# A two-block fp32 model on one core: the cross-attention memory loaded features-first, its 1/rms moved to keys and values, and the second attention's values projected at the start

## The chip, the cores and the metric

The kernel runs on one core of a Trainium2 chip. The metric is the device time of one launch, in microseconds (us), the median of several executions. Lower is better.

## What is computed

A batch of one sequence of 256 tokens with 1024 features goes through two models in a row. The first is one block: adaptive modulation of a hybrid mixer (a state-space scan beside causal attention) and a feed-forward. The second has two layers, each with a SwiGLU feed-forward, a mixer (layer 0: trailing means, layer 1: native sparse attention, NSA), a cross-attention to a memory of 256 tokens, and another feed-forward. The change is about that memory, the input `mem_2` of 256 x 1024:

```python
def rms_norm_2(x, g):
    xf = x.astype(F32)
    y = xf * lax.rsqrt(jnp.mean(xf * xf, axis=-1, keepdims=True) + EPS)
    return (y * g.astype(F32)).astype(x.dtype)

def memory_cross_attention(h, mem_n, w_q, w_kv, w_o):
    q = (h @ w_q).astype(F32).reshape(B, S, Hx, dh) * dh ** -0.5
    k, v = jnp.split((mem_n @ w_kv).astype(F32), 2, axis=-1)
    p = jax.nn.softmax(jnp.einsum('bqhd,bkhd->bhqk', q, k), axis=-1)
    o = jnp.einsum('bhqk,bkhd->bqhd', p, v).reshape(B, S, D)
    return o.astype(h.dtype) @ w_o

for i in range(2):
    ...
    x = x + memory_cross_attention(rms_norm_2(x, xattn_norm[i]), rms_norm_2(mem, mem_norm[i]),
                                   xattn_w_q[i], xattn_w_kv[i], xattn_w_o[i])
```

The memory does not depend on `x`, so its keys K and values V of either layer (called K0, V0, K1, V1 here) can be computed at any time before they are used. The 1/rms of a memory token is one number per token; the gain `mem_norm` is one number per feature and layer. A factor per token passes through the projection `mem_n @ w_kv` unchanged.

## The kernel before

**fp32 as three products.** Every fp32 operand of a large matmul is split in two parts, hi (ACT, a cast, L183 for weights and L393 for activations) and lo (DVE or POOL, the difference, L184 and L394). A product is then three matmuls (hi by hi, lo by hi, hi by lo), all issued in `mm`, L232.

**Weights.** The class `Weights` (object `W`) holds the list of all weight tiles in the order of use. Each is 1 MB (128 x 2048), loaded by SP at L166 into one of four raw tiles `w`, and then split in four pieces of 128 x 512 into `hi` and `lo`. `W.get` hands out a tile and emits the loads and splits of the next two. The modulation's weights, `ada`, are not split: DVE multiplies them with a row of the conditioning (`crow`, in tile `xn`) and sums, two instructions of 128 x 1024 for each (L581).

**A granule** is here one weight tile of the memory's projection, 256 output columns over all 1024 features and 256 tokens: 48 matmuls of 128 x 256 into one PSUM bank of the pair `wk`. K of a layer is granules 0 to 3 of `xkv`, V is granules 4 to 7. `kv_proj` runs them and hands each result to a function `put`.

**The start.** SP loads the two halves of the memory tokens-first into `x0` and `x1` (L319), and then weight tiles in the order "KAKAKAKAAKAKAKAK" (K a granule of xkv, A one of ada). DVE sums squares by token (L539), POOL takes the power -1/2 (L542), DVE scales (L543), PE transposes 16 blocks (L401), and `gained` multiplies with layer 0's gain (L408) and splits into `memT[0]`. Then come K0's four granules; layer 1's gain is put on the same transposed blocks (`memT[1]`); then K1's four granules. `put` copies a granule out of PSUM on ACT (L569). The input `xT` is loaded behind the first granule of K1. Then the first block's input is modulated (L599, tile `A`) and its projections begin (tiles `hTh`, `hTl`, first matmul `ck<-hTh,m`).

**Spills.** K0, K1 and both `memT` pairs (four MB for these) go to DRAM in the first block, by DMAs on ACT's queue (`spill_mem`, `spill_more`, `spill_rest`), since their SBUF tiles are needed. In the first block stands also the matmul pair `ck<-aa,gt`, which takes the decays that DVE computes up to L727.

**Later uses.** POOL loads `memT[0]` back before the first mixer of the second model, where V0's four granules run (`v_keep`, ACT copies at L1324) beside the trailing means (L1302 to L1320). POOL loads `memT[1]` back (`mem_load(1)`) in NSA, and V1's four granules run there as a filler of the attention (`wk<-hi,s` and `wk<-lo,s`, ACT copies at L1572), with their four weight tiles.

**NSA.** For each of two groups `o_` run `nq_proj`, `compressed` and `branches`. `branches` has 8 heads; each has `scores` (12 matmuls with `acc` as output, row maxima on DVE at L1518 and L1519, exponentials on ACT) and, one head later, `values`: three transposes of the probabilities for each token half (L1537 to L1539, the first of the pairs is called T here), copies on ACT (L1540), 12 instructions `ck<-A,m` of 65 columns, and on DVE the scaling by the gates (L1548 to L1551). POOL adds the result to `on` (tile `A`, L1554 and L1555). `turned` transposes `on` (L1581) and splits it for the output projection `nwo`, whose first half has the two `nwo` tiles (outputs `wk`, added to `x` at L1594) and whose second half is `out_tail` (outputs `acc`).

**What sets the order.** The order of the instructions on each engine is fixed when the program is built. A scheduler in the build takes the instructions, their dependences and estimated costs, and puts matmuls that need nothing of the attention between its steps. PE cannot choose at run time: if the next matmul in its list waits, all behind it wait.

Of the kernel before, what the change touches and what calls it, by code (L numbers as in the profile page):

```python
# [9 lines left out]
F32 = mybir.dt.float32  # L10
# [3 lines left out]
OP = mybir.AluOpType  # L14
# [50 lines left out]
def lay_out(i):  # L65
# [4 lines left out]
    o["mem"] = np.ascontiguousarray(a["mem_2"][0])  # L70
# [128 lines left out]
def tile_model(ctx: ExitStack, tc: tile.TileContext, I, out):  # L199
# [80 lines left out]
    j = i = 0  # L280
    for ch in "KAKAKAKAAKAKAKAK":
        if ch == "K":
            add(f"xkv{j // 4}", j % 4, j % 4 + 1, I["xkv"][j // 4])
            j += 1
        else:
            add_ada(i)
            i += 1
# [23 lines left out]
    add("xkv1", 4, 8, I["xkv"][1])  # L311
# [207 lines left out]
    memd = [[dp.tile([P, 2048], F32, name=f"memd{l}{i}") for i in range(2)] for l in range(2)]  # L519
    memps = []  # L520
    memT = [pair_tile(("s8_0", "s8_1")), pair_tile(("s8_2", "s8_4"))]
    jk = sb("s8_4", [P, D], BF16)
# [25 lines left out]
    with tc.issue_after(last["hi"].ins), tc.issue_after(last["lo"].ins):  # L548
        W.emit(1)
# [14 lines left out]
    def k_hold(l):  # L564
        k_held.append([sb(f"x{h}", [P, 4, S]) for h in range(2)] if l == 0 else [sb("s8_3", [P, 8, S])])

        def put(j, ps):
# [76 lines left out]
    def spill(dst, src):  # L644
# [1016 lines left out]
```

## Time and profile before

| | us |
|---|---|
| median of 3 runs (lowest, highest) | 1628.38 (1624.29, 1629.59) |
| the profiled execution, as timed | 1626.63 |
| its span, first to last instruction | 1624.9 |
| PE busy | 1582.5 (97%) |
| DVE busy | 1063.9 (65%) |
| ACT busy | 836.6 (51%) |
| POOL busy | 261.5 (16%) |
| DMA traffic | 304.21 MB, mean 187 GB/s |
| mean granted TensorE clock | 0.993 of full |

The profiled execution lies 1.75 us under the median of the three. Times of instructions count from the start of the span. PE's busy time covers matmuls that overlap in the pipeline, so a matmul of 0.28 us may start every 0.12 us, and a short wait can hide in it; what counts on PE is the distance between starts. In a timeline the bracket at a row's end holds the idle time before it and what released it.

### The profile page before, as it was taken

The numbers are of one execution on the slowest core, as the hardware profiler recorded it, in microseconds if no ns is written. First come the engines' busy times: TensorE is split into PE (matmuls) and PEld (weight loads), VectorE is DVE, ScalarE is ACT, GpSimd is POOL, SyncE is SP. The second block draws the span as 40 slices with busy tenths as digits, with TensorE's granted clock in tenths as the row PEclk, the third lists the DMA queues.
The fourth block names the chain that finished last, engine by engine and source line by source line (L and its number), as shares of the span: only waits on it lengthen the run. The fifth ranks groups of instructions, "written<-read, shape, count | busy, mean of one in ns | idle before, by whom it ended". The sixth has DMA issues, their size and how long they took to land.

```text
span 1624.9 us, 29581 instructions
## 1 busy us (share of the span) xinstructions
PE 1582.5 (97%) x12110; PEld 1514.5 (93%) x12110; DVE 1063.9 (65%) x1938; ACT 836.6 (51%) x1720; POOL 261.5 (16%) x266
## 2 busy tenths in 40 slices
PE   7999999899999999999999999999999999999998
PEld 7999998798988999989999999999989999999897
DVE  8889977874548655586665457544678566575453
ACT  4565446364535544465554445443546675464442
POOL 2003002320301110130121012201200211022011
PEclk9999999999999999999999999999999999999999
DMA  8874766475545555524365545544445223365530
GB/s 321 335 290 154 295 249 221 151 278 203 182 156 208 208 182 208 182 104 182 130 227 188 183 156 208 182 182 156 178 171 207 79 104 131 130 222 185 197 136 27
DMA packets 43432, 304.21 MB, mean 187 GB/s; under 512 B 5008, under 2 KB 5264, under 8 KB 7328
## 3 DMA queue, kind: packets, MB, share of 16 engines
q1 hardware_dynamic: 39312, 283.66, 48.3%
q0 software_dynamic: 2112, 10.49, 1.8%
q10 hardware_dynamic: 1872, 8.17, 1.3%
q8 instruction: 95, 1.56, 0.4%
q14 instruction: 41, 0.34, 0.1%
HBM read 294.96 MB, written 7.34 MB: 186 GB/s over the span
## 4 chain that ended last, share of the span: by engine, by line
PE 62%; DVE 4%; ACT 2%; issue 1%; POOL 0%; POOLq 0%; DVEq 0%; ACTq 0%
PE wk L232 21%; PE ck L232 20%; PE acc L232 19%; DVE lo L184 1%; ACT hi L183 1%; DVE s L1411 0%; DVE m L1307 0%; PE ck L1537 0%; DVE hTl L1045 0%; PE ck L1538 0%; PE ck L1539 0%; ACT s L183 0%; DVE m L408 0%; PE ck L1265 0%; DVE hTl L394 0%
## 5 line engine op out<-in xcount | busy, mean ns | idle before, releaser
L183 ACT CAST hi<-w 128x512 fp32r<-128x512 f32 (+1 forms) x708 | 417.0, 644 | 406.5 <-issue 251.2
L184 DVE TENSOR_TENSOR lo<-w,hi 128x512 fp32r<-128x512 f32 (+1 forms) x708 | 496.8, 745 | 147.8 <-ACT hi L183 144.1
L232 PE MATMUL wk<-hTl,hi 128*128 128x256 f32 x992 | 281.3, 284 | 1.5 <-DVE hTl L1045 1.5
L232 PE MATMUL wk<-hTh,hi 128*128 128x256 f32 x992 | 282.5, 285 | 0.0
L232 PE MATMUL wk<-hTh,lo 128*128 128x256 f32 x992 | 281.1, 283 | 0.0
L394 POOL TENSOR_TENSOR A<-m,A 128x256 fp32r<-128x256 f32 x119 | 135.7, 1146 | 666.3 <-ACT A L393 653.2
L183 ACT CAST s<-w 128x512 fp32r<-128x512 f32 x224 | 126.1, 617 | 138.5 <-issue 85.3
L232 PEld LDWEIGHTS wk<-hTl,hi 128*128 128x128 f32 x992 | 187.5, 189 | 2.7 <-DVE hTl L1045 1.9
L232 PEld LDWEIGHTS wk<-hTh,hi 128*128 128x128 f32 x992 | 187.5, 189 | 0.9 <-issue 0.2
L232 PEld LDWEIGHTS wk<-hTh,lo 128*128 128x128 f32 x992 | 187.2, 189 | 0.1
L232 PE MATMUL acc<-A,hi 128*128 128x256 f32 x1024 | 185.2, 283 | 0.9 <-ACT A L393 0.9
L184 DVE TENSOR_TENSOR s<-w,s 128x512 fp32r<-128x512 f32 x224 | 146.3, 697 | 53.5 <-ACT s L183 51.6
L232 PEld LDWEIGHTS acc<-A,hi 128*128 128x128 f32 x1024 | 157.0, 189 | 1.4 <-ACT A L393 1.1
L232 PE MATMUL ck<-hTh,hi 128*128 128x256 f32 x528 | 149.1, 282 | 0.0
L232 PE MATMUL ck<-hTh,lo 128*128 128x256 f32 x528 | 148.7, 282 | 0.0
L232 PE MATMUL ck<-hTl,hi 128*128 128x256 f32 x528 | 148.7, 282 | 0.0
L232 PE MATMUL acc<-A,lo 128*128 128x256 f32 x512 | 143.3, 280 | 0.0
L232 PE MATMUL acc<-hi,A 128*128 128x512 f32 x432 | 139.9, 398 | 0.0
L232 PE MATMUL ck<-hTh,s 128*128 128x256 f32 x672 | 123.7, 282 | 0.0
L232 PEld LDWEIGHTS ck<-hTh,s 128*128 128x128 f32 x672 | 105.5, 190 | 0.0
L232 PEld LDWEIGHTS ck<-hTh,hi 128*128 128x128 f32 x528 | 99.5, 188 | 0.1
L232 PEld LDWEIGHTS ck<-hTl,hi 128*128 128x128 f32 x528 | 99.4, 188 | 0.1
(407 smaller groups left out, 3162.7 us busy)
## 6 DMA issues: line engine op xcount, KB each, us to landing
w<-in_ffn_i SPq DMA_DIRECT2D x88, 1024.0 KB, 4.8
w<-in_ffn_o SPq DMA_DIRECT2D x44, 1024.0 KB, 4.8
w<-in_ada SPq DMA_DIRECT2D x24, 1024.0 KB, 5.5
w<-in_win SPq DMA_DIRECT2D x22, 1024.0 KB, 7.1
w<-in_xkv SPq DMA_DIRECT2D x16, 1024.0 KB, 6.2
w<-in_ffi SPq DMA_DIRECT2D x16, 1024.0 KB, 4.8
w<-in_ffo SPq DMA_DIRECT2D x16, 1024.0 KB, 4.8
w<-in_nin SPq DMA_DIRECT2D x10, 1024.0 KB, 4.8
```

Source lines behind the costliest of these rows:

```text
L183: nc.scalar.copy(h[:, sl], t[:, sl])
L184: nc.vector.tensor_tensor(lo[:, sl], t[:, sl], h[:, sl].bitcast(F32), op=OP.subtract)
L232: T.matmul(o, lhsT=lhsT, rhs=rhs, start=start, stop=stop)
L394: i = (lo or V).tensor_tensor(dst[1], src, dst[0].bitcast(F32), op=OP.subtract)
```

## The change

`mem_2` is laid out features-first on the host and loaded as `mraw` (two DMAs of 512 KB into `hTh`). There are no transposes at the start. `mem_gain(l)` puts a layer's gain on it: for each of 8 feature blocks an ACT instruction of 128 x 256 (hi) and a DVE instruction (lo). `mem_sums` computes the 1/rms: two ACT squares of 128 x 1024, 16 one-column matmuls against ones, a DVE instruction, POOL's power into `mcol` (a column by token), two matmuls that turn it into a row in PSUM and an ACT copy into `mrow`. Keys are multiplied by the row when they leave PSUM (DVE, in place of the ACT copy), values by the column (two ACT instructions in place of one copy). The order at the start is K1, V1, K0, with 12 granules in place of 8 and the same 8 `ada` tiles. V1 is spilled to DRAM (`vd`) and loaded back by one POOL DMA where its projection stood in NSA. Of the memory only layer 0's pair is spilled.

```diff
@@ -67,7 +67,7 @@
-    o["mem"] = np.ascontiguousarray(a["mem_2"][0])
+    o["memT"] = np.ascontiguousarray(a["mem_2"][0].T.reshape(8, P, S).transpose(1, 0, 2)).reshape(P, 8 * S)
@@ -277,11 +277,12 @@
-    j = i = 0
-    for ch in "KAKAKAKAAKAKAKAK":
+    early = [("xkv1", j) for j in range(8)] + [("xkv0", j) for j in range(4)]
+    i = 0
+    for ch in "KKAKAKKAKAKAKAKKAKAK":
         if ch == "K":
-            add(f"xkv{j // 4}", j % 4, j % 4 + 1, I["xkv"][j // 4])
-            j += 1
+            name, j = early.pop(0)
+            add(name, j, j + 1, I["xkv"][int(name[-1])])
...
     add("nin", 6, 10)
-    add("xkv1", 4, 8, I["xkv"][1])
     add("nwo", 0, 4)
...
-    mt = [sb(f"x{t}", [P, D]) for t in range(2)]
-    for t in range(2):
-        nc.sync.dma_start(mt[t], I["mem"][TS[t]])
+    mraw = sb("hTh", [P, 8, S])
+    for h in range(2):
+        nc.sync.dma_start(mraw[:, 4 * h:4 * h + 4].rearrange("p k s -> p (k s)"), I["memT"][:, h * 1024:h * 1024 + 1024])
...
-    for t in range(2):
-        ss = stat(2)
-        V.scalar_tensor_tensor(jk, mt[t], 1.0, mt[t], op0=OP.mult, op1=OP.mult, accum_out=ss[:, 0:1])
-        ms, rs = stat(), stat()
-        V.tensor_scalar(ms, ss[:, 0:1], D * 1e-6, None, op0=OP.add)
-        G.tensor_tensor(rs, ms, mhalf, op=OP.pow)
-        V.tensor_scalar(mt[t], mt[t], rs, 32.0, op0=OP.mult, op1=OP.mult)
-    for t in range(2):
-        ps = transposes(mt[t], t)
-        gained(ps, t, memT[0], vec("mem_norm0"))
-        memps.append(ps)
...
+    def mem_gain(l):
+
+        for k in range(8):
+            g = vec(f"mem_norm{l}", k)
+            A.activation(memT[l][0][:, k], mraw[:, k], AF.Copy, scale=g)
+            V.scalar_tensor_tensor(memT[l][1][:, k], mraw[:, k], g, memT[l][0][:, k].bitcast(F32), op0=OP.mult, op1=OP.subtract)
+
+    mcol = cp.tile([P, 2], F32, name="mcol")
+    mrow = sb("rrow", [P, S], bufs=2)
+
+    def mem_sums():
+        sq = sb("hTl", [P, 8, S])
+        for h in range(2):
+            A.activation(sq[:, 4 * h:4 * h + 4], mraw[:, 4 * h:4 * h + 4], AF.Square)
+        ps = ck((P, 2))
+        for t in range(2):
+            for k in range(8):
+                mm(ps[:, t:t + 1], sq[:, k, TS[t]], ones[:, 0:1], start=k == 0, stop=k == 7)
+        ms = stat(2)
+        V.tensor_scalar(ms, ps, 1.0 / D, 1e-6, op0=OP.mult, op1=OP.add)
+        G.tensor_tensor(mcol, ms, mhalf.broadcast_to([P, 2]), op=OP.pow)
+        ps = ck((P, S))
+        for t in range(2):
+            mm(ps[:, TS[t]], mcol[:, t:t + 1].broadcast_to([P, P]), ident)
+        A.copy(mrow, ps)
+
+    mem_gain(1)
...
         def put(j, ps):
-            n = 4 // len(k_held[l])
-            A.copy(k_held[l][j // n if n < 4 else 0][:, 2 * (j % n):2 * (j % n) + 2], ps)
             if l == 1 and j == 0:
-                tc.keep_in_program_order(A.dma_start(xT, I["xT"].rearrange("p (k t) -> p k t", k=8)))
+                mem_sums()
+            n = 4 // len(tiles)
+            V.tensor_tensor(tiles[j // n if n < 4 else 0][:, 2 * (j % n):2 * (j % n) + 2], ps,
+                            mrow.unsqueeze(1).broadcast_to([P, 2, S]), op=OP.mult)
+        return put
+
+    def v_put(vt, after=None):
+        def put(j, ps):
+            for t in range(2):
+                A.activation(vt[:, t, (j - 4) * 256:(j - 4) * 256 + 256], ps[:, t], AF.Copy, scale=mcol[:, t:t + 1])
+            if after and j == 4:
+                after()
         return put
...
+    kv_proj(1, k_hold(1), 0, 4)
+    mem_gain(0)
+    v1 = A0([P, 2, D])
+    kv_proj(1, v_put(v1, lambda: tc.keep_in_program_order(A.dma_start(xT, I["xT"].rearrange("p (k t) -> p k t", k=8)))), 4, 8)
+    spill(kd[1], k_held[0][0])
+    spill(vd, v1)
     kv_proj(0, k_hold(0), 0, 4)
-    for t in range(2):
-        gained(memps[t], t, memT[1], vec("mem_norm1"))
-    kv_proj(1, k_hold(1), 0, 4)
...
-    spill_rest()
...
-    mem_load(1)
...
-    kv_proj(1, v1_keep, 4, 8)
+    G.dma_start(KV[1][1].rearrange("p t d -> p (t d)"), vd)
```

DVE at the start: L543 scales the memory, L408 and L394 make the gained pair, L581 (now L607) is the first `ada` step, `lo_199` (now `lo_150`) the first weight tile's lo parts. Before:

```order
L408 TENSOR_TENSOR m_30_192<-acc_171,vecs 128x256
L394 TENSOR_TENSOR s_1_6_111<-m_29_188,s_0_5_110 128x2x128
L581 SCALAR_TENSOR_TENSOR w_211,modc<-w_211,xn_117 128x1024
L184 TENSOR_TENSOR lo_199<-w_196,hi_198 128x512 x4
L184 TENSOR_TENSOR lo_216<-w_213,hi_215 128x512 x4
```

Now:

```order
L541 SCALAR_TENSOR_TENSOR s_4_7_111<-hTh_67,vecs,s_2_6_110 128x256 x8
L184 TENSOR_TENSOR lo_150<-w_147,hi_149 128x512 x4
L184 TENSOR_TENSOR lo_162<-w_159,hi_161 128x512 x4
L607 SCALAR_TENSOR_TENSOR w_171,modc<-w_171,xn_114 128x1024 x2
L555 TENSOR_SCALAR stat_242<-ck_225 128x2
L541 SCALAR_TENSOR_TENSOR s_1_5_109<-hTh_67,vecs,s_0_4_108 128x256 x3
```

The first `ada` step moved from ahead of the first granule's lo parts to behind the second's.

PE in NSA, in the attention heads of the first group, from a head's first T to the next head's values. L1537 to L1539 and their new numbers L1554 to L1556 are the transposes, `wk_14576` is V1's granule 4, `wk_14786` a part of the turned attention output. Before:

```order
L1537 MATMUL ck_13872<-ident,m_731_13824 128x128
L1538 MATMUL ck_13872<-ident,m_731_13824 128x128
L1539 MATMUL ck_13872<-ident,m_731_13824 128x128
L232 LDWEIGHTS identb
L232 MATMUL acc_13897<-negm,identb 128x2x128
L232 MATMUL wk_14576<-hi_14050,s_1_675_13392 128x256
L232 MATMUL wk_14576<-hi_14050,s_0_674_13391 128x256
L232 MATMUL wk_14576<-lo_14051,s_0_674_13391 128x256
```

Now:

```order
L1554 MATMUL ck_14168<-ident,m_731_14120 128x128
L1555 MATMUL ck_14168<-ident,m_731_14120 128x128
L1556 MATMUL ck_14168<-ident,m_731_14120 128x128
L232 LDWEIGHTS identb
L232 MATMUL acc_14193<-negm,identb 128x2x128
L1595 MATMUL wk_14786<-ident,A_624_13067 128x128 x2
L1554 MATMUL ck_14173<-ident,m_731_14120 128x128
```

Behind the last row of the piece before come 15 more matmuls of V1 and then the head's second T; now there are one or two transposes of the turned output, or nothing, between the two T. The next piece is DVE in attention heads without V1: L1519 (now L1536) is the row maximum of the wider scores of the next head, L1551 (now L1568) the scaling that frees the `ck` bank which the second T writes. Before, in a head of the second group:

```order
L1518 TENSOR_REDUCE stat_14376<-acc_14368 128x2
L1548 RECIPROCAL rv_14319<-ck_14312 128x4
L1549 TENSOR_TENSOR rv_14319<-rv_14319,gates_12866 128x4
L1551 TENSOR_TENSOR m_823_14322<-ck_14312,rv_14319 128x256
L1519 TENSOR_REDUCE stat_14376<-acc_14369 128x2
```

Now, in a head of the first group:

```order
L1535 TENSOR_REDUCE stat_14116<-acc_14108 128x2
L184 TENSOR_TENSOR lo_14796<-w_14793,hi_14795 128x512
L1565 RECIPROCAL rv_14059<-ck_14052 128x4
L1536 TENSOR_REDUCE stat_14116<-acc_14109 128x2
L1566 TENSOR_TENSOR rv_14059<-rv_14059,gates_13082 128x4
L184 TENSOR_TENSOR lo_14796<-w_14793,hi_14795 128x512
L1568 TENSOR_TENSOR m_717_14062<-ck_14052,rv_14059 128x256
```

The maximum has moved ahead of the scaling, as in four of the first group's heads.

## Rows read from the trace of the kernel before

**Rows 1.** The page of the profile: busy time by engine (us, share of the span, instructions), and the share of the span of each engine in the chain that ended last.

```profile
PE 1582.5 (97%) x12110; PEld 1514.5 (93%) x12110; DVE 1063.9 (65%) x1938; ACT 836.6 (51%) x1720; POOL 261.5 (16%) x266
...
PE 62%; DVE 4%; ACT 2%; issue 1%; POOL 0%; POOLq 0%; DVEq 0%; ACTq 0%
```

**Rows 2.** What PE waited for over the whole span: the waiting output and line, the releaser, us in total, times, longest.

```profile
PE wk L232 <- ACT hi L183: 3.7, 1, 3.7
PE wk L232 <- DVE lo L184: 3.3, 3, 1.7
PE acc L232 <- ACT hTh L1317: 2.6, 1, 2.6
...
PE ck L232 <- DVE x L727: 1.5, 1, 1.5
```

**Rows 3.** Stretches of the span: from:to, length, busy us of PE, PEld, DVE, ACT and POOL (instructions), granted clock, DMA share, GB/s.

```profile
10.00:20.00 10.00, 4.92 (x28) 4.24 (x28) 10.00 (x21) 7.10 (x16) 3.92 (x4) 0.85 0.81 339
...
20.00:68.00 48.00, 46.32 (x389) 45.96 (x389) 46.87 (x84) 25.89 (x49) 4.52 (x4) 1.00 0.97 373
```

**Rows 4.** PE's timeline from the first granule to the end of K1: start, us, line, operation, idle time before it.

```profile
15.61 0.51 PE L232 MATMUL wk<-s,hi 128*128 128x256 f32 x2 [3.71 <-ACT hi L183]
17.45 0.58 PE L232 MATMUL wk<-s,lo 128*128 128x256 f32 x1 [1.33 <-DVE lo L184]
...
20.39 0.40 PE L232 MATMUL wk<-s,hi 128*128 128x256 f32 x2
...
43.70 0.39 PE L232 MATMUL wk<-s,lo 128*128 128x256 f32 x1 [1.68 <-DVE lo L184]
...
66.08 0.28 PE L232 MATMUL ck<-hTh,m 128*32 128x256 f32 x1
```

**Rows 5.** The timelines of ACT and of DVE at the start.

```profile
14.95 4.25 ACT L183 CAST hi<-w 128x512 fp32r<-128x512 f32 x8
15.06 1.21 DVE L581 SCALAR_TENSOR_TENSOR w<-w,xn 128x1024 f32<-128x1024 f32 x1
16.20 3.00 DVE L184 TENSOR_TENSOR lo<-w,hi 128x512 fp32r<-128x512 f32 x4
```

**Rows 6.** ACT's copies of the first four granules, each started when its granule's last matmul had ended.

```profile
24.54 0.59 ACT L569 COPY x<-wk 128x512 f32<-128x512 f32 x1 [5.34 <-PE wk L232]
30.30 0.59 ACT L569 COPY x<-wk 128x512 f32<-128x512 f32 x1 [2.79 <-PE wk L232]
```

**Rows 7.** Groups of instructions in the first 75 us, shapes kept apart: count, busy us, mean ns of one, idle before.

```profile
L184 DVE TENSOR_TENSOR lo<-w,hi 128x512 fp32r<-128x512 f32 x32 | 20.9, 714 | 0.5 <-ACT hi L183 0.5
L581 DVE SCALAR_TENSOR_TENSOR w<-w,xn 128x1024 f32<-128x1024 f32 x16 | 19.9, 1281 | 0.0
...
L408 DVE TENSOR_TENSOR m<-acc,vecs 128x256 f32<-128x256 f32 x16 | 5.9, 411 | 0.0
...
L542 POOL TENSOR_TENSOR stat<-stat,mhalf 128x1 f32<-128x1 f32 x2 | 1.1, 566 | 4.3 <-DVE stat L541 4.3
```

**Rows 8.** The DMAs issued between 1.5 and 2.0 us on SP's queue: transfers, KB each, us from issue to landing.

```profile
w<-in_xkv SPq DMA_DIRECT2D x1, 1024.0 KB, 9.9
x<-in_mem SPq DMA_DIRECT2D x1, 512.0 KB, 6.1
```

**Rows 9.** PE's timeline around the decays of the scan.

```profile
114.56 0.40 PE L232 MATMUL ck<-aa,gt 128*128 128x16 f32 x2 [1.49 <-DVE x L727]
114.81 0.37 PE L232 MATMUL ck<-aa,le 128*128 128x16 f32 x2
...
116.15 0.42 PE L232 MATMUL wk<-lo,hTh 128*128 128x256 f32 x1
...
119.35 0.29 PE L232 MATMUL wk<-lo,hTh 128*128 128x256 f32 x1
```

**Rows 10.** ACT's timeline where V0 is projected: instructions of the trailing means, and one copy of V0.

```profile
704.20 0.51 ACT L1320 ACTIVATE x<-x,psb 128x256 f32<-128x256 f32 x1
...
706.40 0.57 ACT L1324 COPY s<-wk 128x512 f32<-128x512 f32 x1
```

**Rows 11.** PE's timeline in NSA: the first T of heads with V1 between (1262.31, 1293.36) and without (1319.08, 1322.80), a second T (1324.09), and the first matmul behind the last values of the first group (1296.47).

```profile
1262.31 0.28 PE L1537 MATMUL ck<-ident,m 128*128 128x128 f32 x1
...
1293.36 0.28 PE L1537 MATMUL ck<-ident,m 128*128 128x128 f32 x1
...
1296.47 1.03 PE L232 MATMUL ck<-kc,s 128*128 128x32 f32 x8
...
1319.08 0.28 PE L1537 MATMUL ck<-ident,m 128*128 128x128 f32 x1
...
1322.80 0.28 PE L1537 MATMUL ck<-ident,m 128*128 128x128 f32 x1
...
1324.09 0.30 PE L1537 MATMUL ck<-ident,m 128*128 128x128 f32 x1 [0.24 <-DVE m L1551]
```

**Rows 12.** DVE's timeline in a head without V1.

```profile
1323.86 0.68 DVE L1519 TENSOR_REDUCE stat<-acc 128x2 f32<-128x512 f32 x1
```

**Rows 13.** POOL's last addition to the first group's output.

```profile
1298.19 0.46 POOL L1555 TENSOR_TENSOR A<-A,m 128x128 f32<-128x128 f32 x1
```

**Rows 14.** Later stretches, columns as in [rows 3]: one with a wait of PE of 1.96 us, and one of heads of which several have no V1 between.

```profile
1200.00:1212.00 12.00, 9.05 (x60) 8.39 (x60) 11.84 (x19) 6.03 (x10) 0.00 (x0) 0.86 0.23 81
...
1312.00:1345.00 33.00, 32.59 (x269) 30.67 (x268) 20.40 (x54) 23.96 (x54) 8.47 (x15) 1.00 0.27 100
```

More of the change, by code (lines that the diff above doesn't have):

```diff
@@ L518, in tile_model @@
     kd = [dp.tile([P, 2048], F32, name=f"kd{i}") for i in range(2)]
-    memd = [[dp.tile([P, 2048], F32, name=f"memd{l}{i}") for i in range(2)] for l in range(2)]
-    memps = []
+    vd = dp.tile([P, 2048], F32, name="vd")
+    memd = [dp.tile([P, 2048], F32, name=f"memd{i}") for i in range(2)]
     memT = [pair_tile(("s8_0", "s8_1")), pair_tile(("s8_2", "s8_4"))]
-    jk = sb("s8_4", [P, D], BF16)
     csil = cp.tile([P, 8], F32, name="csil")
@@ L535, in tile_model, with spill @@
     row_of(crow, csil)
-    for t in range(2):
-        ss = stat(2)
-        V.scalar_tensor_tensor(jk, mt[t], 1.0, mt[t], op0=OP.mult, op1=OP.mult, accum_out=ss[:, 0:1])
-        ms, rs = stat(), stat()
-        V.tensor_scalar(ms, ss[:, 0:1], D * 1e-6, None, op0=OP.add)
-        G.tensor_tensor(rs, ms, mhalf, op=OP.pow)
-        V.tensor_scalar(mt[t], mt[t], rs, 32.0, op0=OP.mult, op1=OP.mult)
-    for t in range(2):
-        ps = transposes(mt[t], t)
-        gained(ps, t, memT[0], vec("mem_norm0"))
-        memps.append(ps)
-    with tc.issue_after(last["hi"].ins), tc.issue_after(last["lo"].ins):
-        W.emit(1)
+    def mem_gain(l):
[21 more added lines that the diff above has]
+    mem_gain(1)
+    def spill(dst, src):
+        tc.keep_in_program_order(A.dma_start(dst, src.rearrange("p k s -> p (k s)")))
     def kv_proj(l, put, lo=0, hi=8):
@@ L642, in conv_chunk @@
         A.activation(cv[:, j], cv[:, j], AF.Silu)
-    def spill(dst, src):
-        tc.keep_in_program_order(A.dma_start(dst, src.rearrange("p k s -> p (k s)")))
     def spill_mem():
-        spill(kd[1], k_held[1][0])
-        spill(memd[0][1], memT[0][1].bitcast(F32))
-        spill(kd[0][:, 0:1024], k_held[0][0])
+        spill(memd[1], memT[0][1].bitcast(F32))
+        spill(kd[0][:, 0:1024], k_held[1][0])
     def spill_more():
-        spill(memd[0][0], memT[0][0].bitcast(F32))
-        spill(kd[0][:, 1024:2048], k_held[0][1])
-    def spill_rest():
-        for i in range(2):
-            spill(memd[1][i], memT[1][i].bitcast(F32))
+        spill(memd[0], memT[0][0].bitcast(F32))
+        spill(kd[0][:, 1024:2048], k_held[1][1])
     def xbc_proj():
@@ L1280, in xattn, with mem_load @@
         out_tail(f"xo{l}", pick(oT, ALL, slice(4, 8)), evac, accs, 2)
-    def mem_load(l):
-        memT[l] = pair_tile(("s8_0", "s8_1"))
+    def mem_load():
+        memT[0] = pair_tile(("s8_0", "s8_1"))
         for i in range(2):
-            G.dma_start(memT[l][i].rearrange("p k s -> p (k s)"), memd[l][i].bitcast(F32R))
+            G.dma_start(memT[0][i].rearrange("p k s -> p (k s)"), memd[i].bitcast(F32R))
     npool = Norm("mix_norm0")
@@ L1290, in tile_model @@
     V.tensor_tensor(psb, vec("pool_b"), vec("pool_scale"), op=OP.mult)
-    ffn("ffn1", 0, n1, add_x_from(npool, n1, 0.5, False), lambda: mem_load(0))
+    ffn("ffn1", 0, n1, add_x_from(npool, n1, 0.5, False), mem_load)
     npool.sums()
@@ L1321, in tile_model @@
     KV[0] = kv_tiles()
-    def v_keep(j, ps):
-        A.copy(KV[0][1][:, :, (j - 4) * 256:(j - 4) * 256 + 256], ps)
+    v_keep = v_put(KV[0][1])
     kv_proj(0, v_keep, 4, 7)
@@ L1569, in tile_model @@
     KV[1] = kv_tiles()
-    def v1_keep(j, ps):
-        A.copy(KV[1][1][:, :, (j - 4) * 256:(j - 4) * 256 + 256], ps)
     G.dma_start(KV[1][0].rearrange("p k s -> p (k s)"), kd[1])
-    kv_proj(1, v1_keep, 4, 8)
+    G.dma_start(KV[1][1].rearrange("p t d -> p (t d)"), vd)
     def turned(o_, dst, fs, ring_):
```

1 line of the change is left out of this document (added).

## The prediction

> **What bounds the kernel now.** I read the page first: PE is busy 97% of the span and takes 62% of the chain that ended last, DVE 4% [rows 1]. So a matmul that PE gets more or less counts in full, and the other engines count only where PE waits for them. The list of waits comes next [rows 2]: in the stages that the change touches PE waits 3.7 us for the first hi part of a weight, 3.3 us in three places for a lo part, 2.6 us for the pool mixer's hTh and 1.5 us for the decays of the scan. Then the two places themselves, in timelines. At the start, between 20 and 68 us, DVE is busy 46.87 of 48 us and the DMA engines 0.97 [rows 3]: that stage has little slack beside PE. In NSA, V1's matmuls fill the gaps of the attention's heads [rows 11], and these the change takes away. The work of PE is nearly the same in both kernels, so the question is at which of the two places V1's 192 matmuls cost more.
>
> **The start.** The first weight lands some 9.9 us after an issue at about 1.7, so at 11.6 [rows 8]. Before, ACT and DVE were busy with the memory then: the first cast starts at 14.95, and DVE does an `ada` step of 1.21 us before the first lo part [rows 5], so that PE begins at 15.61 and flows from 17.45 [rows 4]. Now the gained pair is made from the load alone, which lands by 7.3 (6.1 after about 1.2) [rows 8]: eight DVE instructions of about 0.41 (L408 as the nearest) [rows 7] end near 11, and the first lo part stands at once behind them. Cast 0.53 (4.25 / 8) and lo 0.75 (3.00 / 4) [rows 5] put the flow at 12.9. The clock is at its lower level (1.2 GHz) for the first matmuls, as the distance of starts tells, and reaches 2.4 GHz 4.8 us after the first one (20.39 - 15.61) [rows 4]. With the same spell now, 20 matmuls of 0.21 run until 17.1 and 28 of 0.12 until 20.4. Before, the first granule had ended at 24.5 [rows 6]. Gain 4.1.
>
> **Sums of squares.** Each of 16 products with ones shows as two instructions if they behave as `ck<-aa,gt`, which is one call, two instructions, and 0.25 us to the next start [rows 9]. At that price the 32 and the four of the row cost 4.5; if each call took one instruction, 2.3. I take 3.9, near the first. Then the row waits for a DVE instruction, POOL's power of 0.57 [rows 7] and two hand-overs, about 1.1, with five matmuls (0.6) in front: +0.5, or up to 2 if DVE is behind with its `ada` step, which stands ahead of it.
>
> **Four more granules.** A granule takes 5.76 (30.30 - 24.54) [rows 6]: +23.0. The stall of 1.68 behind the fourth granule [rows 4] I take as gone: 12 granules of lo parts (20.9 / 8 = 2.6 each), the `ada` steps (21), 16 gains (6.6) and eight key scalings (0.68 each, as the 512-column row of [rows 12]) are 64 us of DVE in about 74 us, less dense than before [rows 3, 7]; and 20 MB at the 373 GB/s of [rows 3] need 56 us. Sum of the first stage: 23.0 - 4.1 - 1.7 + 3.9 + 0.5 = +21.6. If the stall stays, +23.3.
>
> **The decays.** The wait of 1.49 is followed by a spell at 1.2 GHz until 119.35, some 16 matmuls at 0.21 in place of 0.12 [rows 9]: together 3.0. PE's list now has 96 matmuls between the last transposes of that part and `ck<-aa,gt`, where it had 62, and the two memT[1] spills have gone from the stage. I take the wait and its spell as gone, -3.1; if the decays are late again, 0.
>
> **V0.** Two scaled ACT instructions replace a copy of 0.57. The nearest row for one is 0.51 for 256 columns [rows 10], so a granule costs ACT +0.4, and three of four lie where PE waits 2.6 for ACT [rows 2]. Between 0 (hidden) and +1.3 (all on the path): +0.5.
>
> **NSA without V1.** By PE's list 94 of V1's matmuls (11.2 us at 0.119) stand between the first T at 1262.31 and the end of the group's last values at 1296.47, the other 98 (11.7) behind that [rows 11]. What they leave is not a shorter head by as much. A head without V1 is seen at 1319.08: it takes 3.72, and its second T waits for the scaling on DVE (L1551) [rows 11]; it is bound by the chain of maximum, exponential, transposes, values and scaling, not by PE. In four heads of the first group DVE's list now has the row maximum of 0.68 [rows 12] ahead of that scaling, which makes 4.4 of 3.72. From 1262.31 to 1293.36 are six heads, 31.05 before; now one of 4.8 (it keeps 16 other matmuls, 1.9 us), three of 4.4 and two of 3.72, together 25.4. So 5.6 of 11.2 are given back. In the second half the output projection takes V1's place as filler, but it can begin only when POOL's last addition is done (1298.65) [rows 13] and then transposes, a cast and a difference have run (about 1.4 more, by 0.53 and 0.75 of [rows 5]), while the matmuls behind the last values start at 1296.47 and last 0.9 [rows 11]: some 2.8 of wait. The last heads of the second group then lack a filler, about 1.1 more. So 7.8 of 11.7 are given back. NSA: -13.4. The bounds are -22.9 (every gap vanishes) and -8 (all eight heads of the second group take 0.68 more too).
>
> **Sum.** +21.6 - 3.1 + 0.5 - 13.4 = +5.6 on the profiled execution of 1626.63, so 1632.2. That execution lies 1.75 under the median of the runs, so I say 1634.0. About 0.3% (4.9 us) is what a measurement of this kernel can tell from no change; the forecast is just beyond it.
>
> **Rivals.** *The clock falls in the unfilled heads.* For it: a wait of 1.96 us leaves 0.86 of 12 us in [rows 14], a loss of 1.7 us, and the 1.49 of [rows 9] was followed by a fall. Against it: 1312 to 1345, which holds heads without V1, shows 1.00 [rows 14], and so does the stretch with the 1.68 wait [rows 3, 4]. With one fall behind the last values and three in the slow heads, 4 x 1.7 = +6.8: about 1641. The Trainium skill ("Perfetto Trace Analysis", Matmul Optimizations) speaks for this rival and against the change: TensorE scales its power with its use, so matmuls should run back to back in batches. The rows agree with it in two of four places.
>
> *The heads close up.* DVE and ACT lose V1's splits (16 of each) and copies in NSA; if that lets a head run at PE's own work of about 2.85 (3.72 less the 0.87 that the chain adds), the first group's six heads take 19 instead of 25.4. For it: the second T waits only 0.24 visibly [rows 11]. Against: the waits of the chain are latencies, which less load does not shorten. Time: 1627.6, no change to be seen.
>
> *The same, and the start better still:* sums at 2.3, and no hand-over wait, as DVE and DMA have slack: another 2 to 2.5 off, and the waits for lo parts (3.3 in three places [rows 2], 1.7 counted) gone too, 1.6. That is 1623.5, faster, and it decides from the point where a head takes less than about 3 us.
>
> *The decays' wait stays or DVE falls behind at the start* (its list has the key scaling between two lo parts): +3.0, about 1637.
>
> **How the numbers follow.** Forecast 0.45, split at the bound into 0.33 slower and 0.12 same; clock 0.13, slower; decays 0.07, slower; heads close up 0.17, same with a small part faster (0.03); with a better start 0.18, faster nearly always (0.17). So faster 0.20, same 0.27, slower 0.53. The forecast's own range is 1630 to 1639. The range for 8 in 10 takes in the clock's and most of the faster case: 1622 to 1643.
>
> **What would show it.** Right: the first granule's matmuls flow from 12 to 13.5 us; K0's last granule ends near 87.5 where the 66.08 row stood; no wait on the decays; first T to first T of 3.7 to 4.4 us in the first group's heads; a PE wait of 2 to 3.5 us on the turned output behind the last values; granted clock 1.00 in NSA. Wrong: heads at 3 us or less, or a clock below 0.95 over the 40 us of the first group's attention, or a DVE-bound first stage, with waits for lo parts in each granule.

## The result and the profile after

The kernel after took 1648.12 us (median of four runs, 1642.96 to 1653.23), the kernel before 1627.55 on the same chip: a ratio of 1.0126, with an interval of 1.0108 to 1.0145. So it is slower by some 20 us, where 1634.0 was forecast and 1643 was the upper end of the range. The profiled execution of after took 1648.03 us with a span of 1646.0, 21.1 us more than the span before.

The page, busy time and chain, against [rows 1]:

```profile
PE 1589.9 (97%) x12130; PEld 1518.8 (92%) x12130; DVE 1064.4 (65%) x1931; ACT 837.5 (51%) x1723; POOL 251.6 (15%) x256
...
PE 58%; DVE 5%; issue 2%; ACT 2%; POOL 1%; POOLq 0%; DVEq 0%; ACTq 0%
```

PE has 20 instructions more and is busy 7.4 us longer, a third of the 21.1; the rest is time in which PE is idle. The list of PE's waits over the whole span (in total, times, longest), which answers to [rows 2]:

```profile
PE ck L1554 <- DVE m L1568: 4.7, 6, 1.4
PE wk L232 <- ACT hi L183: 4.0, 1, 4.0
PE wk L1595 <- POOL A L1572: 3.9, 6, 1.2
PE ck L1554 <- DVE stat L1537: 3.8, 3, 1.9
...
PE acc L232 <- DVE A L711: 1.6, 1, 1.6
...
PE ck L232 <- ACT hTh L393: 1.2, 1, 1.2
...
PE wk L232 <- ACT A L668: 0.9, 1, 0.9
```

The wait for a lo part in the granules and the one on the decays have gone. Three new lines (L1554 twice, L1595) belong to NSA: 12.4 us together, where before 0.2 stood on the second T. Of these 7.7 lie in the six heads of the first group shown below (5.9 on DVE, 1.8 on POOL), 1.2 behind that group's last values and 3.5 in the second group.

The start on PE, in order of time, against [rows 4]:

```profile
13.08 0.79 PE L232 MATMUL wk<-s,hi 128*128 128x256 f32 x2 [4.02 <-ACT hi L183]
...
17.15 0.28 PE L232 MATMUL wk<-s,lo 128*128 128x256 f32 x1
...
20.81 3.96 PE L232 MATMUL ck<-ones,hTl 128*128 128x1 f32 x32
24.63 0.78 PE L232 MATMUL wk<-s,hi 128*128 128x256 f32 x2
...
26.00 1.23 PE L232 MATMUL ck<-ident,mcol 128*128 128x128 f32 x4
26.87 0.56 PE L232 MATMUL wk<-s,lo 128*128 128x256 f32 x1
...
30.83 0.28 PE L232 MATMUL wk<-s,lo 128*128 128x256 f32 x1
```

The granules flow from 13.08. Their matmuls start 0.21 us apart until 17.15, as at the lower clock (1.2 GHz), and 0.12 apart, as at the full one (2.4 GHz), until the sums begin at 20.81; the column of the granted clock shows 1.00 for all of this stretch, so that the slow spell is read from the distance of the starts alone. The sums are 32 instructions in 3.8 us. Behind them a matmul takes 0.21 us again instead of 0.12, until 30.8, and here the column shows it too (0.52 over 24 to 31 us, in the windows below). So the one-column sums do not only cost their own time: the clock falls while they run.

The end of the last granule and the hand-over to the modulation:

```profile
90.86 0.28 PE L232 MATMUL wk<-s,lo 128*128 128x256 f32 x1
92.31 0.31 PE L232 MATMUL ck<-hTh,m 128*32 128x256 f32 x1 [1.17 <-ACT hTh L393]
93.22 0.30 PE L232 MATMUL ck<-hTl,m 128*32 128x256 f32 x1 [0.61 <-DVE hTl L394]
```

The matmul that stood at 66.08 now starts at 92.31, 26.2 later.

NSA's first group, first T's of the heads (and what happens in the slow ones), against [rows 11]:

```profile
1286.14 0.28 PE L1554 MATMUL ck<-ident,m 128*128 128x128 f32 x1
...
1293.94 0.33 PE L1595 MATMUL wk<-ident,A 128*128 128x128 f32 x1 [0.90 <-POOL A L1572]
...
1296.21 0.28 PE L1554 MATMUL ck<-ident,m 128*128 128x128 f32 x1
...
1298.70 0.30 PE L1554 MATMUL ck<-ident,m 128*128 128x128 f32 x1 [1.88 <-DVE stat L1537]
...
1299.88 1.45 PE L232 MATMUL ck<-A,m 128*128 128x65 f32 x12
1301.17 0.28 PE L1554 MATMUL ck<-ident,m 128*128 128x128 f32 x1
...
1303.18 0.30 PE L1554 MATMUL ck<-ident,m 128*128 128x128 f32 x1 [1.41 <-DVE m L1568]
...
1304.15 0.47 PE L1595 MATMUL wk<-ident,A 128*128 128x128 f32 x1 [0.45 <-POOL A L1572]
...
1305.94 2.65 PE L232 MATMUL ck<-A,m 128*128 128x65 f32 x12
1308.40 0.42 PE L1554 MATMUL ck<-ident,m 128*128 128x128 f32 x1
...
1319.55 0.28 PE L1554 MATMUL ck<-ident,m 128*128 128x128 f32 x1
...
1326.78 0.55 PE L232 MATMUL wk<-hTh,hi 128*128 128x256 f32 x1 [1.28 <-DVE hTl L394]
```

The six heads from 1286.14 to 1319.55 take 33.4 us with 87 of V1's matmuls fewer in them; before they took 31.05. A head takes 4.96 at full clock (1296.21 to 1301.17), with 1.88 of it in one wait. The next takes 7.2: its twelve value matmuls last 2.65 us where the head before has 1.45. The windows (busy time and count of PE, PEld, DVE, ACT and POOL, the granted clock, DMA share, GB/s) show the same:

```profile
24.00:31.00 7.00, 7.00 (x33) 6.75 (x34) 5.28 (x10) 3.74 (x8) 0.82 (x1) 0.52 0.36 150
...
1270.00:1300.00 30.00, 26.07 (x198) 22.99 (x197) 21.17 (x56) 20.41 (x46) 3.17 (x6) 1.00 0.26 91
1300.00:1325.00 25.00, 19.14 (x118) 16.55 (x117) 8.17 (x26) 9.82 (x22) 4.54 (x10) 0.78 0.08 33
1325.00:1350.00 25.00, 23.58 (x164) 20.87 (x164) 15.97 (x43) 14.27 (x33) 2.54 (x4) 0.88 0.12 43
```

At 0.78 over 25 us, 5.5 us of clock are missing; at 0.88, 3.0. Together that is 8.5 us, an upper bound of what the falls cost, since a wait for another engine is no longer at a lower clock.

Where the 21.1 us came from can be followed at places that both kernels have, by how much later after reaches them: +26.2 at the first matmul behind the hand-over (66.08 before), +25.5 at the pool mixer behind V0 (724.0), +23.8 at NSA's first T (1257.99), +26.2 at the last head's first T in the first group (1293.36), +27.9 at NSA's last T, +21.8 at the end of the part behind it (1431.5). So the first stage costs 26.2, the decays give back 0.7 and V0 costs nothing. From NSA's first T on, 2.0 are given back of V1's 22.9. The 1.7 between the pool mixer and the first T do not come from V1's place: the kernel below that has V1 back in NSA gains 2.5 there too (+7.8 to +5.3), and loses 2.7 behind it (+8.0 at the end). Why it does was not followed.

### The profile page after: what moved, and what is told of

Read it like the earlier page. It is cut to its first block, busy times and chain, and to the rows that moved or that the text cites. A ratio compares the mean times of both kernels' runs of the same rounds, so it can differ in the third digit from the quotient of the medians.

```text
span 1646.0 us, 29617 instructions
## 1 busy us (share of the span) xinstructions
PE 1589.9 (97%) x12130; PEld 1518.8 (92%) x12130; DVE 1064.4 (65%) x1931; ACT 837.5 (51%) x1723; POOL 251.6 (15%) x256
## 4 chain that ended last, share of the span: by engine, by line
PE 58%; DVE 5%; issue 2%; ACT 2%; POOL 1%; POOLq 0%; DVEq 0%; ACTq 0%
PE ck L232 20%; PE acc L232 19%; PE wk L232 19%; DVE lo L184 1%; ACT hi L183 1%; DVE s L1429 0%; DVE hTl L1065 0%; DVE m L1327 0%; DVE m L1568 0%; PE ck L1554 0%; DVE hTl L394 0%; POOL A L1572 0%; DVE stat L1536 0%; ACT hTh L1064 0%; POOL A L1571 0%
## 5 line engine op out<-in xcount | busy, mean ns | idle before, releaser
L394 POOL TENSOR_TENSOR A<-m,A 128x256 fp32r<-128x256 f32 x119 | 136.0, 1148 | 664.3 <-ACT A L393 662.5
L232 PEld LDWEIGHTS ck<-hTh,lo 128*128 128x128 f32 x528 | 99.7, 189 | 0.0
```

Source lines behind the costliest of these rows:

```text
L232: T.matmul(o, lhsT=lhsT, rhs=rhs, start=start, stop=stop)
L394: i = (lo or V).tensor_tensor(dst[1], src, dst[0].bitcast(F32), op=OP.subtract)
```

## The experiments

The theory at first was that after loses at two places: the sums (by the clock, and the hand-over behind them) and NSA, where the clock falls once V1's matmuls no longer fill the heads. The rival was that the heads are held by the chain of DVE, ACT and POOL alone, and the clock only shows it. The steps below give each run's shift at the places above where it decides.

**V1 back in NSA, the memory still features-first.**

```diff
-    early = [("xkv1", j) for j in range(8)] + [("xkv0", j) for j in range(4)]
-    for ch in "KKAKAKKAKAKAKAKKAKAK":
+    for ch in "KAKAKAKAAKAKAKAK":
...
+    add("xkv1", 4, 8, I["xkv"][1])
...
-    kv_proj(1, v_put(v1, ...), 4, 8)
+    kv_proj(1, v1_keep, 4, 8)
```

> Features-first memory with the sums as in the changed kernel, but V1 projected in NSA as before (K0, K1 at the start, V1's weights and memT[1] loaded late). Theory, place of V1: the changed kernel lost about 19 us because V1's 22.9 us of matmuls filled waits of NSA that stay without them, so with V1 back the time is near before, 1630 (before plus some 2.5 for the start, from the 25.5 us by which the stages behind the start lie later, less 23.0 for four granules). Rival, the features-first memory is itself the cost (scaling on DVE, sums, one more pass): 1640 or more. PE's waits in the first group's heads as before, granted clock 1.00 there.

Measured: 1635.02 us, ratio 1.0044 (1.0028 to 1.006). It is +7.8 at the pool mixer and +8.0 at the end, and the six heads take 31.2 (31.05 before), so on balance NSA is as before. The place of V1 is worth 13 of the 20 us, the form of the memory 7.

**The sums with 128 columns of ones,** in that kernel and in after. The products take the same number of instructions, but each has 128 columns.

```diff
-        ps = ck((P, 2))
+        ps = ck((P, 2, P))
...
-                mm(ps[:, t:t + 1], sq[:, k, TS[t]], ones[:, 0:1], start=k == 0, stop=k == 7)
+                mm(ps[:, t], sq[:, k, TS[t]], ones, start=k == 0, stop=k == 7)
```

> As the kernel with V1 late, but the 16 sums of squares go against 128 columns of ones in place of one (the same sums, 128 times). Theory, the one-column matmuls let the clock fall: the same number of instructions at 0.11 to 0.12 us, no spell at 1.2 GHz behind them, so 3 us less than with V1 late (1627). Rival, the clock falls because of the wait for the row of 1/rms: no difference between the two.

> The changed kernel with the sums against 128 columns of ones. Theory, one-column matmuls let the clock fall: PE at 2.4 GHz from about 17 us on, the second granule done 3 us earlier, 1645. Rival, the wait for the row is to blame: 1648, with a spell at 1.2 GHz behind it.

Measured: 1631.36 (1.0029, 1.0018 to 1.004) with V1 late, and 1643.94 (1.0097, 1.0077 to 1.0117) for after: each some 4 us less for 128 times the columns. The intervals of either pair touch, but both pairs go the same way, and the traces show the reason. In after's version the window of the sums shows the clock at 1.00, where the kernel after had 0.52 over 24 to 31 us. With V1 late it is 1.00 over 24 to 31 as well. Three other kernels of this study have the one-column sums at this place (V1 late, and the two with added matmuls in after below), and in each the granted clock is 0.76 over 24 to 31. So it falls in four of four with one column and in none of two with 128.

```profile
20.00:31.00 11.00, 9.84 (x85) 9.63 (x85) 9.82 (x21) 5.29 (x12) 1.59 (x1) 1.00 0.99 369
...
1275.00:1300.00 25.00, 20.46 (x127) 17.70 (x125) 14.43 (x37) 17.17 (x40) 3.16 (x6) 0.80 0.24 86
1300.00:1325.00 25.00, 18.67 (x104) 15.68 (x105) 8.12 (x25) 8.55 (x19) 4.54 (x10) 0.73 0.00 1
1325.00:1350.00 25.00, 25.00 (x183) 22.77 (x183) 15.35 (x44) 14.98 (x34) 2.55 (x4) 0.93 0.12 43
```

In this profiled execution the first matmul behind the hand-over starts at 89.19 instead of 92.31, and at the pool mixer the gain is 4.8 (+20.7 instead of +25.5). From NSA's first T on nothing is given back: 1.5 are lost (+17.3 to +18.8), and the clock is lower than in after (13.5 us missing in the three windows). That the same instructions meet the clock differently also fits the ten us between after's own runs; what decides when it falls was not followed. With V1 late, PE's longest new wait is 4.0 us for ACT's A (L659). In front of it DVE waits for the spill of a key tile, as its row shows:

```profile
111.03 0.69 DVE L747 TENSOR_TENSOR x<-ck,le 128x512 f32<-128x512 f32 x1 [5.23 <-DMA kd<-x]
```

**The kernel before, without V1's projection.** Its matmuls go, nothing is put in the early part, and the attention takes other data of the same size in V1's place.

```diff
-    add("xkv1", 4, 8, I["xkv"][1])
-    mem_load(1)
-    kv_proj(1, v1_keep, 4, 8)
+    G.dma_start(KV[1][1].rearrange("p t d -> p (t d)"), memd[1][0])
```

> The kernel before without the projection of V1 (its weights, its granules and the second load of the memory are left out, and the attention takes other data of the same size in place of V1). Theory, V1's matmuls filled waits: of 22.9 us of matmuls only some 4 come off, 1623.5, with waits on the scaling, on the row maximum and on POOL's additions in the heads, and a spell at 1.2 GHz. The prediction's term: -13.4, 1614. Rival, all of it was bound by PE: -22.9, 1604.6.

Measured: 1629.24 us, ratio 1.0016 (1.0002 to 1.003). 22.9 us of matmuls leave NSA and nothing is gained: it is +1.1 at the first T and +3.1 at the end of the part behind NSA. The windows of NSA:

```profile
1265.00:1290.00 25.00, 18.43 (x117) 15.68 (x116) 12.43 (x33) 16.37 (x39) 4.98 (x10) 0.84 0.13 43
1290.00:1315.00 25.00, 22.33 (x101) 18.97 (x100) 6.58 (x22) 4.59 (x11) 2.72 (x6) 0.54 0.00 1
```

In the second one PE is busy 22.33 of 25 us with 101 matmuls, at 0.54 of the clock: at full clock it would be idle for about half of it (22.33 x 0.54 is 12, an estimate). 15.5 us of clock are missing in the two. This is the plainest result of the study: beside the heads V1's matmuls were free here, so to move them elsewhere can only cost. They also go with the clock: in each of the eight kernels of this study with V1 in NSA the granted clock is 1.00 through the first group's heads, and in each of the six that have neither V1 nor anything else in its place it falls there.

**Six needless matmuls per head,** in after's first group. They use data that is there, and nothing reads their result.

```diff
+                if o_ == 0 and b == 0:
+                    for _ in range(6):
+                        mm(ps[:, 3], ident, ident)
```

> The changed kernel with six needless matmuls (identity by identity, into a free part of the transposes' bank) behind the first T of each head of the first group: 96 instructions, some 10.6 us of PE work that serves no result. Theory, the heads are bound by their chain and the clock fell for want of matmuls: the work lies in waits, the granted clock stays at 1.00 until 1320, and the time is 1642 to 1646 in place of 1648. Rival, the waits are too short or lie elsewhere: the heads grow by the added work, 1652 or more.

Measured: 1644.44 us, ratio 1.0107 (1.009 to 1.0125), 3.7 less than after, though the two intervals overlap, with some 10.6 us more work on PE (96 instructions at 0.11).

```profile
1300.00:1325.00 25.00, 22.38 (x184) 20.39 (x183) 11.46 (x34) 13.70 (x30) 4.91 (x10) 1.00 0.00 1
```

The clock is 1.00 where after had 0.78, and from NSA's first T on 5.5 are given back instead of 2.0. This speaks for the clock, but the order of the program changed with it: the transposes of L1595, which wait for POOL, went behind the heads in this kernel, and in DVE's list the scaling is ahead of the row maximum again in some heads (at 1292.47 and 1296.93). How much of the 3.5 is theirs can't be told from it.

**The same in both groups, in the kernel before without V1's projection.**

```diff
-                if o_ == 0 and b == 0:
+                if b == 0:
```

> The kernel before without V1's projection (other data in its place) and with six needless matmuls behind the first T of every head of both groups, 192 instructions, some 21 us of PE work. Theory, the clock's fall is the larger part of what the missing V1 costs: the clock stays at 1.00 through the heads, and the time is under the kernel without V1 (1629.2), 1622 to 1626, though PE does 21 us more. Rival, waits of the chain alone: the added work fills them without loss or gain, 1629, or lengthens them, 1635.

Measured: 1629.37 us (1.0016, 1.0007 to 1.0026), the same as without them. 21 us of work came in for nothing; NSA's last T is at +1.5 instead of +9.3 without them. But the output projection's matmuls left the heads for the stretch behind them, which takes the gain back. Inconclusive on the clock; that PE has this much room beside the heads it does show.

**192 needless matmuls put back in NSA of after.**

```diff
+    for j in range(4, 8):
+        W.add(("xkv1", 4 + j), I["xkv"][1][j])
...
+    kv_proj(1, again, 8, 12)
```

> The changed kernel with four granules of matmuls, 192 instructions and 22.9 us of PE work at 2.4 GHz, put back where V1's stood in NSA, with their weights and the load of layer 0's memory; the result is thrown away (V1 still comes from the start). Theory, V1 filled waits and kept the clock up: the time is 1645 to 1651, the same as the changed kernel (1648), the granted clock in the heads 1.00. Rival, part of what was taken away had counted: as much over 1648 as it counts, 1661 if the prediction's 13.4 was right, 1671 if PE alone bounds.

Measured: 1669.92 us, ratio 1.0271 (1.0248 to 1.0294), 22 more than after. It did not test what it was made for: in PE's order only some 82 of them stand in the first group's heads, 14 in the middle and none in the second group's, with the output projection behind the heads as well. The first T is at +20.2 and the last at +17.4, so the heads did gain, and the tail paid. It shows one thing by the way, heads with no filler at all and at full clock:

```profile
1341.16 0.28 PE L1559 MATMUL ck<-ident,m 128*128 128x128 f32 x1
...
1344.88 0.28 PE L1559 MATMUL ck<-ident,m 128*128 128x128 f32 x1
...
1348.63 0.28 PE L1559 MATMUL ck<-ident,m 128*128 128x128 f32 x1
```

They take 3.72 and 3.75 us, which is the 3.72 of the prediction. They are heads of the second group, in which DVE's scaling comes ahead of the row maximum.

**The sum as a row, with POOL's power on 128x256.** The row of 1/rms is then made directly, with no wait for a column. In after, with V1 late, and with the key tiles of V1-late spilled in another order.

```diff
+        ps = ck((P, S))
+        for k in range(8):
+            mm(ps, ones, sq[:, k], start=k == 0, stop=k == 7)
+        V.tensor_scalar(mrow, ps, 1.0 / D, 1e-6, op0=OP.mult, op1=OP.add)
+        G.tensor_tensor(mrow, mrow, mhalf.broadcast_to([P, S]), op=OP.pow)
```

> The changed kernel with the sums turned round: ones is the stationary operand and eight matmuls stream 256 columns of squares, so that the sum comes out as a row; POOL takes the power of the row, and the column is transposed from it later. Nothing on PE waits for the row. Theory: 16 instructions of 0.12 us in place of 32 and a wait, 2 us for the sums in place of 3.9 and 1.2 for the wait, so 3 us under the sums against 128 columns (1643.9): 1641. Rival: POOL's power of 128 x 256 is slow and the keys wait for it, then PE waits for a bank: 1645.

> V1 in NSA as before, features-first memory, sums as a row. Theory: 2 to 3 us under the kernel with V1 late and 128 columns (1631.4): 1629, still some 2 us over before for the wait of 4 us in the first block's convolution behind K0's spill. Rival: the sums are hidden in that wait in both: 1631.

> The same with K0 spilled ahead of K1 and of memT[0]. Theory: DVE's wait of 5.2 us for K0's spill, with PE's 4.0 behind it, goes: 1625, a little under before. Rival: the next spill in the queue is then late for the next tile (s8_3 or s8_0), and the wait only moves: 1629.

Measured: 1688.89 (1.0377), 1670.4 (1.0269) and 1668.54 (1.0256). One row of POOL tells why:

```profile
25.60 42.01 POOL L554 TENSOR_TENSOR rrow<-rrow,mhalf 128x256 f32<-128x256 f32 x1 [21.17 <-DVE rrow L553]
```

The power of 256 columns takes 42 us where one column took 0.57 [rows 7]. DVE waits 41.06 us for it with the key scaling, and all behind that on DVE is late. The price for one column was no guide for 256. The other order of the spills gives 1.9 of 1670 less, which is within the two intervals, and the wait only went to the other tile.

**The sums ahead of the first granule.** Squares and wide sums go where PE waits for the first weight anyway, only the row of 1/rms stays behind the first granule. First into the bank of before (`ck`), in after and with V1 late, there also with the other order of spills.

```diff
+    mem_sums()
     mem_gain(1)
...
-                mem_sums()
+                mem_row()
```

> The changed kernel with the squares and the sums (against 128 columns of ones) ahead of the first granule, where PE waits for the first weight from 9.05 to 13.08 us, and only the row of 1/rms behind it. Theory, the sums cost what they stand in front of: they vanish into that wait, the row no longer waits, and the clock is up when the first granule begins: 4 to 6 us under the sums against 128 columns behind the granule (1643.9), so 1639. Rival, the squares delay the gained pair on ACT and the granule begins 2 us later: 1642.

> V1 in NSA as before and the features-first memory with these early sums. Theory: the start gains 4 to 6 us on the kernel with V1 late and 128 columns (1631.4), 1626, about the time of before; what is left of the loss is the wait of 4 us in the convolution behind K0's spill, and 2 us at the hand-over to hT. Rival, the gain of the start is swallowed by the DMA-bound loads behind it: 1630.

> The same with K0 spilled first. Theory, as with the sums as a row this order takes some 2 us off: 1624, under before (1627). Rival: the wait moves to the next tile and nothing is gained: 1626.

Measured: 1644.98 (1.0114, 1.0098 to 1.0129), 1629.66 (1.0018, 1.0007 to 1.0029) and 1628.65 (1.0014, 1.0005 to 1.0023). In after they still held the start up:

```profile
13.86 6.72 PE L232 MATMUL ck<-ones,hTl 128*128 128x128 f32 x32 [4.77 <-ACT xn L531]
```

They wait 4.77 us until ACT has read the `ck` banks, and the first granule stands behind them in PE's queue, until 20.34. So, the bank alone changed:

```diff
-        ps = ck((P, 2, P))
+        ps = wk((P, 2, P))
```

> The changed kernel with the early sums in a bank of the wk pair, which is free then; in the earlier try they waited until 13.86 us for ACT to empty the ck banks. Theory: the sums run from 9.1 to 13 us, in PE's wait for the first weight, the first granule is at 2.4 GHz from its start, and the time is 5 us under the first try of early sums (1645.0): 1640. Rival, the squares end too late on ACT and the sums begin only at 11: 1642.

> V1 in NSA as before, features-first memory, early sums in the wk bank. Theory: 5 us under the first try (1629.7), 1624 to 1625, under before (1627.0). Rival, the stage behind is bound by its loads and by the wait of 3 to 4 us in the convolution, which takes the gain: 1628.

Measured: 1640.88 (1.0073, 1.0053 to 1.0094) and 1629.16 (1.001, 0.9997 to 1.0022). The start in after's version:

```profile
8.89 4.76 PE L232 MATMUL wk<-ones,hTl 128*128 128x128 f32 x32
13.40 0.49 PE L232 MATMUL wk<-s,hi 128*128 128x256 f32 x2
13.72 0.28 PE L232 MATMUL wk<-s,lo 128*128 128x256 f32 x1
```

The sums stand in a gap that was there, and the first granule runs at the full clock from its first matmul. The first matmul behind the hand-over starts at 83.33, +17.2 now, for 23 us of granules. With V1 late the form of the memory costs nothing that can be measured. These two differ in V1's place and what goes with it (the order of the first granules, V1's spill): 11.7 us. No version beat the kernel before.

In after's version nothing is given back from NSA's first T on (+14.0 to +15.5), and again the clock is low there: 0.75 over 1275 to 1300 and 0.70 over 1300 to 1325.

## Why the prediction was right or wrong

The direction was right, and the size was not: 5.6 us were forecast on the profiled execution, and it grew by 21.4. Of the 15.8 between them NSA has 11.4, the first stage 4.6 and the decays 2.4, while 2.6 went the other way.

**The start: right.** The flow was forecast at 12.9 and is at 13.08; the end of its slow spell at 17.1 and is at 17.15. The stall of 1.68 is gone, as forecast.

**Sums of squares: too small.** 4.4 were forecast, the row and its wait with them. The 32 instructions take 3.8 and the row's four 0.9; what lacked is the fall of the clock behind them. Between 24.63 and 30.83 some 25 matmuls take 0.21 instead of 0.12, 2.4 us. The sum is 7.1, 2.7 more than forecast. That this is the clock and not the work, the two runs with 128 columns show: more columns, 4 us less.

**Four more granules: right in price, but for the hand-over.** The last granule ends at 91.0, where 87.5 was forecast: 2.7 of that are the sums, 0.4 the later end of the first granule. Then the turned hT is late: 1.17 and 0.61 of wait, where PE had none before (the term had nothing for this). DVE reaches it behind the lo parts of the next weights. DVE was taken as having slack in this stage; it has it on the mean, not at its end.

**The decays: the wait is gone, the gain is not.** 3.1 were forecast (3.0 by the rows that it names), and 0.7 remain at the pool mixer. Two waits came in their place, 0.9 on ACT's A (L668) and 1.6 on DVE's A (L711), where the list of before has 0.6. Nothing had been named as late next.

**V0: 0.5 forecast, nothing seen.**

**NSA without V1: the step that failed.** 13.4 were to be given back, and 2.0 were. The six heads were to go from 31.05 to 25.4, and they took 33.4. Behind the last head's first T in that group 7.8 were to be given back, and 4.4 were (+26.2 to +21.8); the wait there, forecast at 2.8, is some 2.5 (1.20 and 1.28). The step had two things wrong in its heads: their length at the full clock, and the clock, which it put at 1.00.

*The length at the full clock.* Four of the six heads ran at 1.00: the first three and the last. By DVE's list, which has the row maximum ahead of the scaling in the first, third, fourth and fifth, they were forecast at 4.8, 3.72, 4.4 and 3.72, and they took 5.2, 4.87, 4.96 and 4.61: 3.0 more. In the second and the last of them stands a wait that no step had, that of the transposes of L1595 for POOL's additions (0.90 and 0.45); before, V1's matmuls lay in front of them. In the head of 4.96 the second T waits 1.88 for DVE, and DVE's rows show why:

```profile
1296.86 0.69 DVE L1536 TENSOR_REDUCE stat<-acc 128x2 f32<-128x512 f32 x1 [0.26 <-PE acc L232]
...
1297.54 0.68 DVE L184 TENSOR_TENSOR lo<-w,hi 128x512 fp32r<-128x512 f32 x1
1298.14 0.41 DVE L1568 TENSOR_TENSOR m<-ck,rv 128x256 f32<-128x256 f32 x1
```

The sum put the row maximum ahead of the scaling (3.72 + 0.68 = 4.4). The list of the new order has a weight's lo part there as well, and with its 0.68 it is 5.1.

*The clock.* Six kernels have these heads without V1 and with nothing in its place: after, its versions with wide sums, with the row and with early sums (two), and the kernel before without V1. Their lists of instructions in the heads are the same on PE, DVE, ACT and POOL, and only the clock meets them at other times, so that a head can be compared with itself. The second, the third and the last of the six in after, each from its first T to the next one's (columns as in the windows above):

```profile
1291.34:1296.21 4.87, 3.39 (x27) 2.78 (x27) 3.92 (x9) 4.87 (x13) 1.35 (x2) 1.00 0.00 0
1296.21:1301.17 4.96, 3.08 (x27) 2.70 (x26) 2.84 (x8) 2.30 (x6) 0.91 (x2) 1.00 0.35 126
1314.94:1319.55 4.61, 3.50 (x29) 2.89 (x28) 0.77 (x3) 0.96 (x2) 0.91 (x2) 1.00 0.00 0
```

The second and the third with wide sums in after:

```profile
1284.74:1291.50 6.76, 5.28 (x28) 4.51 (x27) 3.92 (x9) 5.12 (x13) 1.35 (x2) 0.70 0.00 1
1291.50:1298.45 6.95, 5.07 (x25) 4.33 (x26) 3.05 (x8) 2.54 (x6) 0.91 (x2) 0.55 0.42 151
```

The last in the kernel before without V1:

```profile
1292.36:1299.09 6.73, 6.38 (x27) 5.25 (x28) 0.77 (x3) 0.96 (x2) 0.91 (x2) 0.50 0.01 2
```

DVE and POOL do the same work in nearly the same time, and the waits of the second and third head are the same too (0.58, 0.90 and 1.88 in both kernels). At a clock of 0.70, 0.55 and 0.50 the same heads take 1.9, 2.0 and 2.1 us more. So the clock is a cost of its own, beside the waits.

*The shares.* The fourth and fifth head, 7.23 and 6.54 in after, were seen at the full clock in none of the six. Where the clock is low all through, they take 7.7 and 7.2; less 2.1 each, the six heads would take some 30 us at the full clock. By this estimate some 3 of the 8.0 that the first group took too much are the clock and some 5 the waits; what is sure is that the clock has no more than 5.1, since 10.2 us of after's heads are at the lower clock. The other half of the step fell short by 3.4, and behind the last values 3.4 us of clock are missing. That these are the same us is not shown: the kernels with the features-first memory and V1 in NSA lose 1.7 to 3.1 there as well, at a clock of 1.00. Over the whole of NSA, the six kernels:

| | clock missing in NSA, us | given back from the first T on, us |
|---|---|---|
| after | 8.5 | 2.0 |
| early sums, bank `ck` | 13.7 | -1.4 |
| wide sums | 13.7 | -1.5 |
| early sums, bank `wk` | 13.7 | -1.5 |
| the kernel before without V1 | 15.4 | -2.0 |
| the row | 18.8 | -5.2 |

By this table each us of clock takes away some 0.7 us. Carried on to no missing clock, some 8 would be given back and not 13.4, again an estimate: of the 11.4 that after lacks, some 6 would be the clock and some 5 the rest, the waits above all.

The prediction had the clock among its rivals ("the clock falls in the unfilled heads") with a chance of 0.13 and 6.8 us, about the size that it has here. It named the sign that it would be wrong by, a clock below 0.95 over the 40 us of the first group's attention; 1285 to 1325 has 15 us at 1.00 and 25 at 0.78, which is 0.86. Against the rival it held two stretches at 1.00 [rows 3, 14], but in both PE was busy nearly all the time (46.32 of 48 us, 32.59 of 33), the later one with the output projection as a filler. The Trainium skill ("Perfetto Trace Analysis", Matmul Optimizations) says that TensorE scales its power with its use and wants its matmuls back to back. These runs agree with it: the granted clock is 1.00 in the heads with V1 and 0.78 over 1300 to 1325 in after.

**The other rivals.** The heads did not close up, the start was not better than forecast, and the decays' wait on L727 did not stay.

## What to carry to other kernels

Matmuls that fill the gaps of an attention can be free there, and they can also hold TensorE's clock. Before moving them, ask what the stretch gains without them; here taking 22.9 us out gained nothing. When a head's length is summed up without them, go through the new lists of every engine for what now stands in front, and put a price on the clock. A reduction by one-column matmuls cost more than its own time here, so give it the columns, or better a gap in which PE waits anyway, and look which PSUM bank it has to wait for.

## What the runs showed of the hardware that was not expected

- 32 one-column fp32 instructions took 3.8 us, and the clock fell to 1.2 GHz (0.52 granted over 24 to 31 us in after, 0.76 in three other kernels); with 128 columns it stayed at 2.4 GHz (1.00 in both kernels), and the kernel was 4 us faster.
- The same attention head, with the same lists on all engines, took 4.87 us at a granted clock of 1.00 and 6.76 at 0.70; another took 4.61 at 1.00 and 6.73 at 0.50. The longest wait of PE in the heads in front of the fall in after was 1.88 us.
- POOL's power took 42.01 us for 128x256 and 0.57 for 128x1: some 0.16 us for each column.
- In the kernel before without V1 a window of 25 us has a granted clock of 0.54 with PE busy 22.33 us of it. A busy share near 90% in the profile does not mean that the clock is up; its own column has to be read.
